# Issuing the loads of the last three parts of w_ada from GpSimd instead of SyncE

## The chip, the cores and the metric

The kernel runs on one core of a Trainium2 chip. The core has TensorE (PE, with its weight loads listed as PEld), VectorE (DVE), ScalarE (ACT), GpSimd (POOL) and SyncE (SP), which issues most DMA transfers. The metric is the device time of one execution in microseconds.

## The reference, cut to what matters

One layer of a decoder trunk on x of 1024 tokens by 1024 features. A conditioning vector c gives six vectors of 1024: shift, scale and gate of the mixer, and shift, scale and gate of the FFN.

```python
c_act = jax.nn.silu(c)
ada = c_act @ w_ada[l] + b_ada[l]                       # 1024 x 6144
sh_m, sc_m, g_m, sh_f, sc_f, g_f = jnp.split(ada, 6, axis=-1)
h = modulate(rms_norm(x), sh_m, sc_m)
proj = h @ w_in[l]
...                                                     # token shift
y_rwkv = rwkv7_time_mix(z, ...)                         # 8 heads x 64, a recurrence over the tokens
y_s5 = s5_mix(u, ...)                                   # 32 groups x 16, state space, then a GLU
mix = jnp.concatenate([y_rwkv, y_s5], axis=-1) @ w_out[l]
x = x + g_m[:, None, :] * mix
h = modulate(rms_norm(x), sh_f, sc_f)
ffn = (jax.nn.silu(h @ ffn_w_gate[l]) * (h @ ffn_w_up[l])) @ ffn_w_down[l]
x = x + g_f[:, None, :] * ffn
return rms_norm(x) * final_gain
```

Parts 0 to 2 of `ada` are shift, scale and gate of the mixer; parts 3, 4 and 5 (shift, scale and gate of the FFN) are first needed after the output projection of the first half.

## The kernel before

The tokens are worked in four quarters (`qt`) for the recurrence and in two halves for the output projection and the FFN. The recurrence of a quarter is prepared (`prepare`, `post`: decays, normed keys, the products `pA`, a triangular solve on DVE or POOL whose input goes out to `l_d` and comes back as `LU`, and whose result goes out to `x_d` and is read again before `pG`), then run as a chain of chunks (`chunk`, L1080: products `p1` to `p4`, copies `R` and `U` and the state `ST` on DVE, each needing the one before), then finished (`finishes`: a norm over each head, `pv` and `pg` on PE, result `yhl`).

The adaLN product `c_act @ w_ada` is not done on PE. w_ada is loaded with its rows over the partitions, each 128-row block is multiplied by its column of `cact` and added up in `acc` (`ada_acc`), and PE adds over the partitions (`ada_cols`, L306, tile `pac`), after which DVE adds the bias into `mod` (L307). Parts 0 to 2 are done at the start, with loads of 512 KB. Parts 3 to 5 are done by `ada_steps` in twelve steps of 256 columns. A step issues four loads of 256 KB (L285, tile `wada`, 128x2x256 elements, four buffers, so that each load waits until the step before has read the same buffer) and then adds up eight blocks. In six steps, called mixed here, ACT multiplies (L299) and POOL adds (L300), after a first multiply on DVE (L295); in the other six, which alternate with them, DVE does all eight (L295 once, L297 seven times). The column sums of a step stand two steps behind its loads.

The work around the change is woven in the source by generators that take turns. The S5 GLU (`s5_glu`: `pglu` on PE, `hl_glu`, `zhl`, `ssum` and `yhl` on POOL) and the steps of w_ada (`adg`) are written beside the chunk chains of the first two quarters, `c0` and `c1`:

```python
    weave(c0, (LIM(glg, 20), 3), LIM(adg, 12))
    ...
    weave(LIM(c1, 14), finishes(0), (glg, 1), (adg, 3))
    ads.close()
    ...
    weave(seq(c1, finishes(1)), LIM(o0, 4), LIM(late, 4))
```

`o0` is the output projection of the first half (`outproj`, L1346, PSUM tile `po`). Its four accumulators use the PSUM tags "s", "p", "A" and "G", which `pac` and the GLU use before, so it starts after the last `pac`; with it run the loads of x (L1312), of w_out (`wraw`, L1341) and of y (L1324). `late` is the recurrence of the last two quarters; after `o0` the FFN (`pgate`, `pup`, `pdn`) runs beside it.

The order in which each engine gets its instructions is not the order of the source: when the program is built, a scheduler with a model of each instruction's time orders them engine by engine. Each engine then runs its own list strictly in that order, and a queue's DMA issues stand in the list of the engine that issues them, with their waits.

Of the kernel before, what the change touches and what calls it, by code (L numbers as in the profile page):

```python
# [17 lines left out]
P = 128  # L18
# [11 lines left out]
def kernel(  # L30
# [38 lines left out]
    nc = tc.nc  # L69
    V, S, G, PE = nc.vector, nc.scalar, nc.gpsimd, nc.tensor  # L70
# [206 lines left out]
    rstd_x = const.tile([P, 8], F32, name="rstd_x")  # L277
    tcol = const.tile([P, 8], F32, name="tcol")

    def ada_load(pl, part, j0, n, bufs):  # L280
        c0 = 1024 * part + 128 * j0
        wts = []
        for kk in range(4):
            wt = pl.tile([P, 2, 128 * n], F32, tag="wada", bufs=bufs, name="wada")
            nc.sync.dma_start(wt, w_ada[0, 256 * kk:256 * kk + 256, c0:c0 + 128 * n].rearrange("(k p) n -> p k n", p=P))  # L285
            wts.append(wt)
        return wts

    def ada_acc(pl, wts, n, eng=V):

        acc = pl.tile([P, 128 * n], F32, tag="acc", bufs=2 if n > 2 else 3, name="acc")
        for k in range(8):
            wt = wts[k // 2][:, k % 2, :]
            if k == 0:
                V.tensor_scalar_mul(acc, wt, cact[:, 0:1])  # L295
            elif eng is V:
                V.scalar_tensor_tensor(out=acc, in0=wt, scalar=cact[:, k:k + 1], in1=acc, op0=ALU.mult, op1=ALU.add)  # L297
            else:
                S.mul(wt, wt, cact[:, k:k + 1])  # L299
                G.tensor_tensor(out=acc, in0=acc, in1=wt, op=ALU.add)  # L300
        return acc

    def ada_cols(acc, part, j0, n, ps):

        for j in range(n):
            PE.matmul(ps[:, j:j + 1], lhsT=acc[:, 128 * j:128 * j + 128], rhs=ones[:, 0:1], start=True, stop=True)  # L306
        V.scalar_tensor_tensor(out=mod[:, part, j0:j0 + n], in0=ps, scalar=1.0 if part in (1, 4) else 0.0,  # L307
                               in1=col("b_ada", 8 * part + j0, n), op0=ALU.add, op1=ALU.add)
# [227 lines left out]

    xts, uw = [load_x(0)], []
    wa = [ada_load(sp, part, 0, 4, 6) for part in range(2)]
    dgs = norm_x(0, xts[0])
    acs = [ada_acc(sp, w, 4) for w in wa]  # L540
    transpose_x(xts[0], dgs)
    uw += [load_u(0), load_u(1)]
    xts.append(load_x(1))
    wa = [ada_load(sp, part, 4, 4, 6) for part in range(2)]
    mods(*acs, 0)
    for b in range(4):
# [17 lines left out]
    for hf, b in ((0, 2), (0, 3), (1, 2)):  # L564
        for k in range(4):
            u_mm(hf, k, b)
    mods(*acs, 4)
    wa = [(part, j0, ada_load(sp, part, j0, 4, 6)) for part in (2,) for j0 in (0, 4)]
    for hf in range(2):
        for k in range(4, 8):  # L570
# [273 lines left out]
    def ada_steps(pl, parts, ps, mix=lambda j: j % 4):  # L844

        todo = []
        def cols():
            acc, part, j = todo.pop(0)
            ada_cols(acc, part, j, 2, ps("pac2")[:, 0:2])
        for part in parts:  # L850
            for j in (0, 2, 4, 6):
                todo.append((ada_acc(pl, ada_load(pl, part, j, 2, 4), 2, V if mix(j) else None), part, j))
                if len(todo) > 2:
                    cols()
                yield
        while todo:
            cols()
            yield
# [244 lines left out]
    def chains(qt):  # L1103
        for ch in range(4):
            gen = [chunk(q, ch, sts[qt, q]) for q in range(2)]
            for _ in range(4):
                for g in gen:
                    next(g)
                yield
# [158 lines left out]
    c0 = chains(0)  # L1268
# [7 lines left out]
    xpa = pool("xpa", stack=xs0)  # L1276
    glg = s5_glu(pool("glp", stack=gls))
    adg = ada_steps(pool("adp2", stack=ads), (3, 4, 5), ps_s)
    weave(c0, (LIM(glg, 20), 3), LIM(adg, 12))

# [239 lines left out]
```

## Time and profile before

| | us |
|---|---|
| median of 3 runs | 1576.38 |
| lowest and highest run | 1573.71, 1582.4 |
| profiled execution | 1568.54 |
| its span, first to last instruction | 1566.8 |
| PE busy | 1415.5 (90%) |
| DVE busy | 939.1 (60%) |
| ACT busy | 568.3 (36%) |
| POOL busy | 540.6 (35%) |

The profile is one execution. Busy time is the sum of an engine's instructions, without DMA issues and waits; a share of the span is a mean over stages with different limits. In the rows further down, times are microseconds from the start of the span unless marked ns, "x" counts instructions, "SPq" is SyncE issuing a transfer, and the text behind an arrow names what released a waiting instruction. The stage of `ada_steps` lies between 430 and 583 us.

### The profile page before, as it was taken

What the parts mean: (1) busy time and instruction counts of PE and PEld (TensorE: products, weight loads), DVE (VectorE), ACT (ScalarE), POOL (GpSimd) and SP (SyncE); (2) the same over time, 40 slices, a digit from 0 to 9 for tenths busy, and PEclk for the clock granted to TensorE, in tenths of its full rate; (3) what the DMA queues carried; (4) which work ended last, traced back from release to release, by engine and by line L of the source; (5) the groups of instructions that cost most, each with busy time, mean ns of one, the idle gap of its engine ahead of it and who ended that gap; (6) DMA issues with size and microseconds to landing.
All of it is one profiled execution on the core that took longest, in us unless ns stands there. A gap on an engine that the chain in (4) does not pass through costs nothing.

```text
span 1566.8 us, 23019 instructions
## 1 busy us (share of the span) xinstructions
PE 1415.5 (90%) x9071; PEld 1142.7 (73%) x9071; DVE 939.1 (60%) x1603; ACT 568.3 (36%) x928; POOL 540.6 (35%) x495
## 2 busy tenths in 40 slices
PE   3897799898968889898999999899997999999997
PEld 2776687676757658686777778777786888888885
DVE  5976328889696877754466755356637433433335
ACT  4342335454346544332143413223443322222223
POOL 4359534342163533371000005200541344544443
PEclk9898899998879859998999999999999999999999
DMA  9734555453463572344123234322822333333331
GB/s 289 227 104 141 167 175 166 115 152 96 90 167 76 148 219 81 81 102 102 45 87 98 81 91 107 85 82 76 246 82 73 116 108 94 95 94 95 108 95 54
DMA packets 261518, 184.54 MB, mean 118 GB/s; under 512 B 79767, under 2 KB 230945, under 8 KB 261409
## 3 DMA queue, kind: packets, MB, share of 16 engines
q1 hardware_dynamic: 257680, 174.85, 38.5%
q10 hardware_dynamic: 2912, 7.64, 1.4%
q8 instruction: 71, 1.16, 0.3%
q0 software_dynamic: 816, 0.57, 0.2%
q14 instruction: 39, 0.31, 0.1%
HBM read 155.53 MB, written 29.59 MB: 118 GB/s over the span
## 4 chain that ended last, share of the span: by engine, by line
PE 63%; DVE 14%; DMA 8%; POOL 7%; ACT 4%; issue 3%; SPq 1%; ACTq 0%; DVEq 0%; POOLq 0%
PE pdn L270 13%; PE pgate L270 13%; PE pup L270 13%; PE pz L270 6%; PE po L1346 5%; PE p L1080 2%; DMA wada<-in_w_ada_dram 2%; PE pu L367 2%; POOL stmp L1024 2%; POOL XU L1026 2%; DVE acc L297 2%; PE pY L765 1%; PE pA L980 1%; DMA LU<-l_d 1%; DVE stmp L1024 1%
## 5 line engine op out<-in xcount | busy, mean ns | idle before, releaser
L270 PE MATMUL pdn<-wd,act 128*128 128x512 f32 x1056 | 271.2, 398 | 0.7 <-DVE x L1395 0.5
L270 PE MATMUL pup<-h,hl_up 128*128 128x512 f32 x1056 | 265.5, 394 | 3.9 <-ACT hl_up L131 3.9
L270 PE MATMUL pgate<-h,hl_g 128*128 128x512 f32 x1056 | 263.4, 395 | 2.3 <-ACT hl_g L131 1.7
L270 PEld LDWEIGHTS pup<-h,hl_up 128*128 128x128 f32 x1056 | 197.0, 188 | 49.1 <-ACT hl_up L131 5.2
L270 PEld LDWEIGHTS pdn<-wd,act 128*128 128x128 f32 x1056 | 197.8, 190 | 46.5 <-DVE x L1395 2.1
L270 PEld LDWEIGHTS pgate<-h,hl_g 128*128 128x128 f32 x1056 | 196.7, 188 | 47.2 <-ACT hl_g L131 3.0
L1395 DVE TENSOR_TENSOR x<-pdn,x 128x512 f32<-128x512 f32 x176 | 118.8, 688 | 185.6 <-PE pdn L270 185.5
L270 PE MATMUL pz<-hT,hl_z 128*128 128x256 f32 (+1 forms) x912 | 188.3, 365 | 24.7 <-POOL hl_z L127 8.1
L270 PEld LDWEIGHTS pz<-hT,hl_z 128*128 128x128 f32 x912 | 153.6, 210 | 55.1 <-ACT zo L890 10.0
L1430 DVE TENSOR_TENSOR rawd<-rawd,gfb 128x1024 f32<-128x1024 f32 x44 | 57.1, 1297 | 91.7 <-DMA rawd<-in_ffn_w_down_dram 65.4
L1346 PE MATMUL po<-wo,yhl 128*128 128x512 f32 x384 | 95.6, 401 | 0.7 <-POOL wo L127 0.7
L131 ACT CAST hl_up<-raw_up 128x1024 fp32r<-128x1024 f32 x44 | 46.2, 1049 | 129.9 <-PE pup L270 103.3
L131 ACT CAST wd<-rawd 128x1024 fp32r<-128x1024 f32 x44 | 45.6, 1049 | 108.7 <-DVE rawd L1430 83.7
L1346 PEld LDWEIGHTS po<-wo,yhl 128*128 128x128 f32 x384 | 71.8, 190 | 18.1 <-issue 1.4
L1424 ACT ACTIVATE sgt<-pgate 128x512 f32<-128x512 f32 x44 | 26.3, 598 | 145.3 <-PE pgate L270 145.1
L1024 POOL TENSOR_TENSOR stmp<-LU,XU 128x126 f32<-128x126 f32 (+22 forms) x62 | 31.0, 500 | 129.3 <-DMA LU<-l_d 124.7
L127 POOL TENSOR_TENSOR hl_g<-raw_g,hl_g 128x1024 fp32r<-128x1024 f32 x19 | 45.6, 2398 | 79.6 <-ACT hl_g L131 75.8
L127 POOL TENSOR_TENSOR wd<-rawd,wd 128x1024 fp32r<-128x1024 f32 x19 | 49.7, 2618 | 55.9 <-ACT wd L131 55.9
L893 POOL TENSOR_TENSOR zo<-zo,zm 128x512 f32<-128x512 f32 x28 | 44.0, 1570 | 70.3 <-ACT zo L890 58.3
L127 POOL TENSOR_TENSOR hl_up<-raw_up,hl_up 128x1024 fp32r<-128x1024 f32 x19 | 49.7, 2616 | 50.6 <-ACT hl_up L131 50.6
L131 ACT CAST hl_g<-raw_g 128x1024 fp32r<-128x1024 f32 x44 | 46.0, 1045 | 48.3 <-DMA raw_g<-in_ffn_w_gate_dram 48.3
L297 DVE SCALAR_TENSOR_TENSOR acc<-wada,cact,acc 128x512 f32<-128x512 f32 (+1 forms) x84 | 62.2, 746 | 1.6 <-DMA wada<-in_w_ada_dram 0.9
(378 smaller groups left out, 2406.0 us busy)
## 6 DMA issues: line engine op xcount, KB each, us to landing
raw_g<-in_ffn_w_gate_dram SPq DMA_DIRECT2D x44, 512.0 KB, 3.9
raw_up<-in_ffn_w_up_dram SPq DMA_DIRECT2D x44, 512.0 KB, 4.3
rawd<-in_ffn_w_down_dram SPq DMA_DIRECT2D x44, 512.0 KB, 3.4
wada<-in_w_ada_dram SPq DMA_DIRECT2D x24, 512.0 KB, 8.8
raw_z<-in_w_in_dram SPq DMA_DIRECT2D x24, 512.0 KB, 5.7
wada<-in_w_ada_dram SPq DMA_DIRECT2D x48, 256.0 KB, 3.1
wraw<-in_w_out_dram SPq DMA_DIRECT2D x32, 256.0 KB, 3.2
zt_d<-zo SPq DMA_DIRECT2D x28, 256.0 KB, 2.9
```

The costliest lines, as they stand in the source:

```text
L127: (eng or G).tensor_tensor(out=out, in0=a, in1=b, op=ALU.subtract)
L131: S.copy(dst[:, 0], src)
L270: PE.matmul(ps, lhsT=lf(a, k), rhs=rf(b, k), start=(n == 0), stop=(n == 3 * kb - 1))
L297: V.scalar_tensor_tensor(out=acc, in0=wt, scalar=cact[:, k:k + 1], in1=acc, op0=ALU.mult, op1=ALU.add)
L367: PE.matmul(pu[hf, b], lhsT=uw[b][:, a_, k, :], rhs=hT[hf, k][:, b_, :], start=(k == 0 and n == 0), stop=(k == 7 and n == 2))
L893: G.tensor_tensor(out=o, in0=o, in1=zm[:, 0:HT], op=ALU.add)
L1024: SOLVE.tensor_tensor(out=t, in0=LU[:, j, j + 1:32].unsqueeze(2).to_broadcast([P, nt, nk]), in1=X[:, j:j + 1, 0:nk].to_broadcast([P, nt, n ...
L1026: SOLVE.tensor_tensor(out=X[:, j + 1:32, 0:nk], in0=X[:, j + 1:32, 0:nk], in1=t, op=ALU.add)
L1080: PE.matmul(ps[r, h], lhsT=a, rhs=b, start=(n == 0), stop=(n == len(ops) - 1))
L1346: PE.matmul(pss[i], lhsT=yh[k][:, a, 128 * i:128 * i + 128], rhs=wo[:, b], start=(k == 4 and n == 0), stop=(k == 3 and n == 2))
L1395: V.tensor_tensor(out=t, in0=ps, in1=t, op=ALU.add)
L1430: V.tensor_tensor(out=raw, in0=raw, in1=gfb, op=ALU.mult)
```

## The change

`ada_load` takes the queue as an argument, and `ada_steps` passes GpSimd's. The 24 loads of parts 0 to 2 stay on SyncE; the 48 loads of 256 KB go to GpSimd.

```diff
-    def ada_load(pl, part, j0, n, bufs):
+    def ada_load(pl, part, j0, n, bufs, q=None):
...
             wt = pl.tile([P, 2, 128 * n], F32, tag="wada", bufs=bufs, name="wada")
-            nc.sync.dma_start(wt, w_ada[0, 256 * kk:256 * kk + 256, c0:c0 + 128 * n].rearrange("(k p) n -> p k n", p=P))
+            (q or nc.sync).dma_start(wt, w_ada[0, 256 * kk:256 * kk + 256, c0:c0 + 128 * n].rearrange("(k p) n -> p k n", p=P))
...
-                todo.append((ada_acc(pl, ada_load(pl, part, j, 2, 4), 2, V if mix(j) else None), part, j))
+                todo.append((ada_acc(pl, ada_load(pl, part, j, 2, 4, nc.gpsimd), 2, V if mix(j) else None), part, j))
```

Since the scheduler orders the whole program anew, the lists of all engines change in this stage. Three places show it.

**POOL, in the second quarter's chain** (`ssum`, `zhl` and `yhl` are the GLU's). Before:

```order
L1017 MEMSET XU 128x512
L1019 MEMSET XU 64x16 x2
L127 TENSOR_TENSOR yhl<-zz,yhl 128x64x4 x4
L814 TENSOR_TENSOR ssum<-ssum,sg 128x256 x3
L127 TENSOR_TENSOR zhl<-zz,zhl 128x1024
L127 TENSOR_TENSOR yhl<-zz,yhl 128x64x4 x4
L300 TENSOR_TENSOR acc<-acc,wada 128x256
```

After:

```order
L1019 MEMSET XU 64x16 x2
L285 DMA wada<-in_w_ada_dram 128x2x256
L127 TENSOR_TENSOR zhl<-zz,zhl 128x1024
L814 TENSOR_TENSOR ssum<-ssum,sg 128x256
L127 TENSOR_TENSOR yhl<-zz,yhl 128x64x4 x4
L814 TENSOR_TENSOR ssum<-ssum,sg 128x256 x2
L127 TENSOR_TENSOR zhl<-zz,zhl 128x1024
L814 TENSOR_TENSOR ssum<-ssum,sg 128x256
L285 DMA wada<-in_w_ada_dram 128x2x256 x4
L127 TENSOR_TENSOR yhl<-zz,yhl 128x64x4 x4
L300 TENSOR_TENSOR acc<-acc,wada 128x256
```

Issues of L285, each with a wait for the reader of its buffer, stand between and ahead of the GLU's work and the adds.

**DVE, around the last state `ST` of the second quarter's chunk chain** (p_5219 is that chunk's product; the number behind `pac` tells the twelve column sums apart). Before:

```order
L297 SCALAR_TENSOR_TENSOR acc<-wada,cact,acc 128x256
L295 TENSOR_SCALAR acc<-wada,cact 128x256
L297 SCALAR_TENSOR_TENSOR acc<-wada,cact,acc 128x256 x2
L1093 TENSOR_TENSOR ST<-p_5219,ST 128x128
L1094 TENSOR_TENSOR ST<-ST,pc 128x128
L295 TENSOR_SCALAR acc<-wada,cact 128x256
L297 SCALAR_TENSOR_TENSOR acc<-wada,cact,acc 128x256
L307 SCALAR_TENSOR_TENSOR mod<-pac_4837,cols 128x2
```

After:

```order
L1093 TENSOR_TENSOR ST<-p_5219,ST 128x128
L253 SCALAR_TENSOR_TENSOR ra<-ra,rs 128x256
L1094 TENSOR_TENSOR ST<-ST,pc 128x128
L254 SCALAR_TENSOR_TENSOR rs<-ra,rs 128x256
L307 SCALAR_TENSOR_TENSOR mod<-pac_4652,cols 128x2
L295 TENSOR_SCALAR acc<-wada,cact 128x256
L830 SCALAR_TENSOR_TENSOR zz<-zz,hga,rs 128x256 x4
L297 SCALAR_TENSOR_TENSOR acc<-wada,cact,acc 128x256
```

The chain's last state stood ahead of the tenth column sum (pac_4837) and stands now ahead of the fifth (pac_4652); behind it the multiply of L295 occurred once more before, and occurs five times now.

**PE, from the last chunk products (p_5308) to the output projection.** Before:

```order
L1080 MATMUL p_5308<-ar,ST 64x64 x2
L1080 MATMUL p_5308<-ak,U 64x64 x2
L919 MATMUL pw<-wzk,wa_132 128x256 x2
L306 MATMUL pac_4837<-ones,acc 128x1 x2
L1117 MATMUL pd<-ar,cen 128x512
L919 MATMUL pa<-wzk,wa_132 128x256 x2
L306 MATMUL pac_4869<-ones,acc 128x1 x2
L1117 MATMUL pd<-ar,cen 128x512
L306 MATMUL pac_4873<-ones,acc 128x1 x2
L1124 MATMUL pv<-lsq,blk 128x512
L1346 MATMUL po<-wo,yhl 128x512 x4
```

After:

```order
L1080 MATMUL p_5308<-ak,U 64x64 x2
L306 MATMUL pac_4652<-ones,acc 128x1 x2
L967 MATMUL pb<-rz,blk 128x512
L1117 MATMUL pd<-ar,cen 128x512
L306 MATMUL pac_4687<-ones,acc 128x1 x2
L919 MATMUL pw<-wzk,wa_132 128x256 x2
L1117 MATMUL pd<-ar,cen 128x512
L306 MATMUL pac_4739<-ones,acc 128x1 x2
L919 MATMUL pa<-wzk,wa_132 128x256 x2
L1124 MATMUL pv<-lsq,blk 128x512
L306 MATMUL pac_4788<-ones,acc 128x1 x2
```

Three column sums stood between the last chunk product and the first `po`; now there are eight, the last four of them (with `pv`, `pg` four times in the list, `pgb` eight times and `pn` between) below the rows shown. Behind that, on PE in the output projection, 16 of the 64 `pA` products of the third quarter stand now ahead of the last 60 `po`, where all 64 stood behind the last `po` before.

## Rows read from the trace of the kernel before

**Rows 1.** The page, busy us (share of the span) and instructions of an engine.
```profile
PE 1415.5 (90%) x9071; PEld 1142.7 (73%) x9071; DVE 939.1 (60%) x1603; ACT 568.3 (36%) x928; POOL 540.6 (35%) x495
```

**Rows 2.** Windows: stretch, length, busy of PE, PEld, DVE, ACT, POOL, clock, DMA, GB/s.
```profile
510.00:550.00 40.00, 33.24 (x410) 25.81 (x408) 34.97 (x80) 20.95 (x44) 19.25 (x21) 0.86 0.57 155
550.00:590.00 40.00, 33.10 (x204) 22.58 (x204) 31.10 (x65) 17.77 (x37) 15.30 (x19) 0.55 0.68 215
...
630.00:670.00 40.00, 33.12 (x268) 26.80 (x267) 28.16 (x53) 12.89 (x25) 12.08 (x8) 1.00 0.36 89
...
720.00:960.00 240.00, 235.77 (x1546) 184.46 (x1545) 144.53 (x214) 76.80 (x106) 3.59 (x11) 0.99 0.31 86
```
**Rows 3.** The chain of waits, 405 to 600 us: start, us, what.
```profile
554.77 8.89 DMA wada<-in_w_ada_dram
564.66 2.74 DMA wada<-in_w_ada_dram
568.84 2.85 DMA wada<-in_w_ada_dram
```

**Rows 4.** Waits of SyncE's queue, 430 to 600 us: total, times, longest.
```profile
SPq L285 <- POOL acc L300: 25.8, 17, 4.2
...
SPq L285 <- DVE acc L297: 7.3, 6, 2.9
```

**Rows 5.** Timeline of PE, 541 to 583 us: start, duration, instruction.
```profile
549.22 1.01 PE L306 MATMUL pac<-ones,acc 128*128 128x1 f32 x4
...
566.89 0.42 PE L1080 MATMUL p<-ak,U 64*64 64x64 f32 x4
...
580.36 0.98 PE L306 MATMUL pac<-ones,acc 128*128 128x1 f32 x4
...
582.64 1.33 PE L1346 MATMUL po<-wo,yhl 128*128 128x512 f32 x1
```

**Rows 6.** The tile wada: ns min/median/max of its issues, and us to landing.
```profile
L285 SPq DMA_DIRECT2D wada<-in_w_ada_dram x72: 367/373/4237, 2.7 to 573.9; - x72
...
DMA to landing us min/median/max: 2.8/3.2/11.7
```

**Rows 7.** The tile dcol, loaded by POOL: the same columns.
```profile
L651 POOL DMA_DIRECT2D dcol<-in_s_d_dram x4: 528/536/568, 129.6 to 131.2; - x4
...
DMA to landing us min/median/max: 2.9/3.2/3.6
```

**Rows 8.** Timeline of POOL at the start of the program.
```profile
2.99 0.60 POOL L315 DMA_DIRECT2D g2w<-in_rw_g_dram  x1
```

**Rows 9.** Timeline of DVE, 128 to 133 us.
```profile
130.31 1.23 DVE L127 TENSOR_TENSOR hl_z<-raw_z,hl_z 128x1024 fp32r<-128x1024 f32 x1
```

**Rows 10.** Groups by line, 430 to 600 us: busy us, mean ns, idle before.
```profile
L300 POOL TENSOR_TENSOR acc<-acc,wada 128x256 f32<-128x256 f32 x42 | 33.7, 803 | 24.5 <-ACT wada L299 21.5 <-DVE acc L295 1.4
...
L297 DVE SCALAR_TENSOR_TENSOR acc<-wada,cact,acc 128x256 f32<-128x256 f32 x42 | 25.5, 608 | 0.4
L299 ACT ACTIVATE wada<-wada,cact 128x256 f32<-128x256 f32 x42 | 19.3, 500 | 24.5 <-DMA wada<-in_w_ada_dram 18.2 <-DVE acc L297 5.2 <-DVE zz L830 0.8
...
L295 DVE TENSOR_SCALAR acc<-wada,cact 128x256 f32<-128x256 f32 x12 | 5.5, 458 | 3.9 <-DMA wada<-in_w_ada_dram 3.9
```

**Rows 11.** Timeline of PE after the first po, 590 to 720 us.
```profile
601.18 1.02 PE L1139 MATMUL pg<-gs,g2w 128*128 128x256 f32 x4
605.71 0.61 PE L1292 MATMUL pgb<-dgb,ones 128*128 128x128 f32 x4
...
619.47 1.02 PE L939 MATMUL pn<-sq,blk 128*128 128x512 f32 x2
...
715.74 1.91 PE L1046 MATMUL pG<-XU,ak 32*32 32x32 f32 x64 [6.71 <-DMA XU<-x_d]
```

## Prediction

> **What bounds the kernel now.** I read the page first, then the busy time by stretch, then the chain of waits, then the waits of SyncE's queue, and last the rows of TensorE where the stage of w_ada ends. The page says that PE is busy 90% of the span [rows 1], but that is a mean. From 720 us on PE works 235.8 of 240 us [rows 2], so what is late there stays late to the end. In 510 to 590 us it works 33.2 and 33.1 of each 40 us, at a granted clock of 0.86 and then 0.55, while DVE works 35.0 of the 40 us up to 550 [rows 2]. That earlier stretch is where the change lies, and there PE waits for others. The chain of waits names the loads of w_ada in it: the three longest pieces at its end are 8.89, 2.74 and 2.85 us [rows 3], the last ahead of the output projection. The queue's own waits say why: before issuing a load of L285 SyncE stood 25.8 us for adds of GpSimd (17 times) and 7.3 us for DVE (6 times), because each of the four buffers has to be read before the next load may fill it [rows 4].
>
> So there are two chains side by side: the twelve steps of w_ada (load, multiply and add, column sums, `mod`), and the chunk chain of the second quarter (L1080). The first output projection `po` takes PSUM tags that the column sums `pac` use, so it starts only after the last `pac`. Its time is the number to forecast. Before, the chunk chain's last group starts at 566.89 us, the last `pac` at 580.36 and the first `po` at 582.64 [rows 5]: 15.75 us from the first of these to the last.
>
> **The change part by part.** The 48 issues leave SyncE. Each costs SyncE 0.37 us (minimum and median 367 and 373 ns), the long ones being waits [rows 6]. That is 48 x 0.37 = 18 us of an engine with nothing else to compute, beside other work: worth nothing by itself. What the queue kept behind it (x, kz, rz, wraw) comes sooner. From the trace that is worth between nothing and the 8.89 us piece [rows 3], whose landing fell beside those loads; I take nothing, as a load that comes sooner has to find PE ready, and below the order says it does not.
>
> GpSimd gets 48 issues. Its other loads are the nearest rows: 0.60 us for the 256 KB of g2w, 528 to 568 ns for the four of dcol, which land in 2.9 to 3.6 us (median 3.2), against 2.8 and 3.2 us for wada on SyncE [rows 6 to 8]. So I take 0.6 us to issue and an unchanged 3.2 us to land. GpSimd now also waits for DVE's release of a buffer before issuing, and what is queued behind it waits too: the adds of the mixed steps (42 of 0.80 us each [rows 10]) and the GLU's `hl_glu`, `ssum`, `zhl` and `yhl`, for which PE and ACT wait.
>
> *The pace of the steps.* A pair is one mixed step and one step on DVE alone. GpSimd pays 8 x 0.6 + 7 x 0.80 = 10.4 us a pair. One buffer's round is two issues and two landings (7.6 us), two DVE operations (1.2 us at 608 ns), an ACT multiply (0.5) and two adds (1.6): 10.9 us [rows 6, 7, 10]. So 5.2 to 5.5 us a step at best. The measured pace before is from the `pac` at 549.22 to that at 580.36, five steps apart: 31.1 / 5 = 6.2 us [rows 5]. I take 6.2, since queueing in the order given comes on top of the bare sums, and keep 5.2 as the lower end.
>
> *What moves behind the chunk chain.* This is the main term, and it comes from the order, not from the queue. The scheduler put the steps of w_ada later against the chunk chain. On DVE, after the chain's last `ST`, before had one and a half steps to go and after has five and a half: four more. On PE three of the twelve `pac` stood after the last L1080 and now eight do. Nothing but small work is left for PE there, so each of these steps is exposed: 4 x 6.2 = 24.8 us (20.8 by the low pace, 31.0 with five steps).
>
> *What the chunk chain gains.* The DVE work of those four steps no longer delays it: two steps of 0.46 + 7 x 0.608 = 4.7 us and two single multiplies of 0.46, 10.3 us [rows 10]. DVE was busy 87% of the time there, so most of it counts, but GpSimd's waits hold the GLU that PE runs in between. Ends: 0 and 10.3 us; I take 7. The chain's last group then starts near 560 us.
>
> *Sum at the first* `po`: 566.9 - 7 + 15.75 + 24.8 = 600.4 us, against 582.64: 17.8 us later.
>
> *What is given back.* While PE waits in the longer tail, it does work that stood behind or among `po` before: `pg` twice 1.02 us, sixteen `pgb` at 0.61 us for four (2.4 us), and `pn` 1.02 us [rows 11]: 5.5 us. Further on PE waited 6.71 us for the solve before `pG` at 715.74 [rows 11]. Preparation for that solve (`pn`, `pb`, a quarter of `pA`) stands earlier against `po` now, so part of this wait goes: from nothing to all, and I take half, 3.4 us. PE's idle 6.9 us in 630 to 670 [rows 2] I leave as it is: the chain from the last `po` through the norm to the first `pgate` still runs there. It is kept for the range. Net: 17.8 - 5.5 - 3.4 = 8.9 us.
>
> The profiled execution took 1568.54 us, its span 1566.8, and stands 7.8 us (0.5%) below the median of 1576.38. The sum against its own time is 1577.4; against the median, 1576.4 + 8.9 = 1585.
>
> The Trainium skill, "DMA: Bandwidth & Descriptors", section "Issuing engines are not separate DMA queues", says that issuing from another engine saves only the issuing time, as all transfers run on the same 16 DMA engines. The landings agree (3.2 us on either path). By that rule alone the change would be worth about nothing; the order's shift is what it leaves out.
>
> **Rivals.**
> *A, given back in full.* The tail is as late as I say or a little less, but the 6.71 us and the 6.9 us of idle PE time go as well, since the preparation runs ahead of `po`. 17.8 - 5.5 - 6.7 - 5 = +0.6 us: 1577. For it: `pA` now starts within `po`. Against it: the wait in 630 to 670 lies partly in DVE and GpSimd work that follows the last `po`.
>
> *B, faster.* The tail is short: the chain ends at 556.6 (all 10.3 us gained) and the four steps take 5.2 us each, so `po` starts at 556.6 + 15.75 + 20.8 = 593.2, 10.5 us late; with 5.5, 6.7 and 5 us given back that is -6.7, and with SyncE's loads early (2.8 us, one landing) about -9: 1567. For it: the waits of SyncE [rows 4] are gone. It decides if the last `pac` comes before about 591 us.
>
> *C, GpSimd's issue is dear.* An issue has to wait until DVE's operation of the moment is done. DVE works 78% of 550 to 590 us (31.1 of 40 [rows 2]) in operations of 0.6 us and more [rows 10], so each issue could take 0.6 us more: 4 issues a step, 2.4 us a step, over the five and a half steps in the tail 13 us more: +22 us, 1598. Against it: the four issues of dcol, from 129.55 us on, all took 528 to 568 ns [rows 7], while DVE ran operations of 1.23 us on 128x1024 elements [rows 9]. It decides if the median issue without its wait is above 1 us. The Trainium skill, "SBUF — State Buffer", section "SBUF: two separate sides", states the mechanism of C: GpSimd writes the descriptors itself and is locked out while DVE runs certain two-port operations; its example goes from about 620 to about 3100 ns. By its figures an issue would cost 2.5 us more, and the sum several tens of us; no row here shows that.
>
> *D, the change does not do what it says* (the loads still on SyncE's queue): the order shows 48 of them on GpSimd, so I give it no weight.
>
> **How the numbers follow.** About 0.5% (8 us) is what a measurement here can tell from no change: faster is below 1568.5, slower above 1584.3. Forecast 0.46, of which 0.35 lies above that bound and 0.11 within; A 0.26, of which 0.24 within and 0.02 below; B 0.16, below; C 0.12, above. So faster 0.18, same 0.35, slower 0.47. The range has to reach A and most of B and C: 1566 at the lower end (B), and at the upper end the sum with five steps and the chunk chain not earlier, 566.9 + 15.75 + 31.0 = 613.7, 31 us late, less 5.5: +25.5, so 1602. The forecast's own range is 1577 to 1593.
>
> **What the profile after would show.** The last L1080 of the second quarter near 560 us (556 to 567); the first `po` near 600 (593 to 614) and after the eighth `pac`; five spacings of `pac` of about 6 us each with PE mostly idle; GpSimd's issues of L285 at about 0.6 us plus waits for DVE; landings near 3.2 us; the wait before `pG` shorter than 6.7 us; PE busy as before from 720 us on. Wrong if `po` starts before 591 us (the tail was hidden), if a bare issue is above 1 us (C), or if `po` is some 18 us late and the end is not (A).

## The result, and the profile after

The changed kernel takes 1612.18 us (median of 4 runs, 1610.82 to 1613.05) against 1579.39 us for the kernel before on the same chip: a ratio of 1.0234, 95% interval 1.0202 to 1.0266. It is 2.3% slower. The forecast was 1585 us, slower too, but the time lies above the whole range (1566 to 1602). The profiled execution took 1612.16 us with a span of 1610.4 us, 43.6 us more than the span of before. The sum had found 8.9 us of that.

The page after, with the line that answers to [rows 1], the line of GpSimd's DMA queue and the line of the loads (KB each, median us to landing):

```profile
span 1610.4 us, 23015 instructions
PE 1437.3 (89%) x9071; PEld 1155.3 (72%) x9071; DVE 950.6 (59%) x1603; ACT 571.2 (35%) x930; POOL 576.4 (36%) x543
q0 software_dynamic: 4656, 13.16, 2.9%
wada<-in_w_ada_dram POOLq DMA_DIRECT2D x48, 256.0 KB, 3.5
```

PE's busy time grew by 21.8 us from [rows 1] with the same 9071 matmuls, nearly all of it in one stretch at a granted clock of 0.50, the lower of its two levels (below); the rest is waiting. By the medians the loss is 32.8 us. The profiled execution of before was a quick one, 10.9 us under the median of its four runs, and that of the changed kernel lies on its median; so about a quarter of the 43.6 us that the traces differ by is spread between executions, and where it lies the traces don't tell. To find the place of the rest, I lined up the same five events in both traces (us from the start of the span):

| event | before | after | later by |
|---|---|---|---|
| solve of the second quarter starts (DVE L1024) | 433.50 | 439.10 | 5.6 |
| its result reaches PE (`pG`) | 478.94 | 485.95 | 7.0 |
| last group of L1080 of that quarter | 566.89 | 571.41 | 4.5 |
| first `po` | 582.64 | 626.81 | 44.2 |
| end | 1566.8 | 1610.4 | 43.6 |

So 39.65 us come up between the last L1080 and the first `po`, and of the 44.2 us by which `po` is late all but 0.6 us reach the end. TensorE's timeline after in that tail (start, length, line, tiles, idle before it and its releaser) answers to [rows 5]:

```profile
571.41 0.42 PE L1080 MATMUL p<-ak,U 64*64 64x64 f32 x4
571.76 1.01 PE L306 MATMUL pac<-ones,acc 128*128 128x1 f32 x4
...
595.37 2.08 PE L1139 MATMUL pg<-gs,g2w 128*128 128x256 f32 x4 [3.03 <-DVE lsq L1125]
603.96 2.08 PE L1139 MATMUL pg<-gs,g2w 128*128 128x256 f32 x4 [6.52 <-DVE ld L1140]
605.83 0.85 PE L306 MATMUL pac<-ones,acc 128*128 128x1 f32 x4
...
621.87 1.01 PE L306 MATMUL pac<-ones,acc 128*128 128x1 f32 x4 [0.66 <-POOL acc L300]
625.22 0.99 PE L306 MATMUL pac<-ones,acc 128*128 128x1 f32 x4 [2.34 <-DVE acc L297]
626.81 0.77 PE L1346 MATMUL po<-wo,yhl 128*128 128x512 f32 x1 [0.60 <-DVE mod L307]
```

Eight `pac` stand behind the last L1080, as the order had said. From the first of them to the last are 53.46 us, 7.64 us a step. The longest waits of PE there end on DVE. The tail by engine (stretch, length, then busy us and instructions of PE, PEld, DVE, ACT and POOL, granted clock, DMA share, GB/s), first before, then after, each with the time from the first `po` to the end behind it:

```profile
566.90:582.60 15.70, 12.62 (x34) 6.83 (x32) 9.15 (x22) 11.08 (x24) 5.22 (x7) 0.50 0.63 185
582.60:1566.80 984.20, 940.76 (x5384) 758.28 (x5382) 515.09 (x747) 308.87 (x468) 286.60 (x242) 0.98 0.33 95
```

```profile
571.40:626.80 55.40, 32.46 (x85) 19.77 (x83) 45.24 (x90) 24.45 (x47) 29.35 (x38) 0.50 0.54 162
626.80:1610.40 983.60, 941.32 (x5354) 756.94 (x5354) 500.15 (x710) 299.81 (x455) 284.07 (x242) 0.98 0.33 95
```

In the tail PE's busy time grew from 12.62 to 32.46 us, at a clock of 0.50 in both, and DVE is busy 45.24 of 55.4 us. Its costliest groups there (operation, tiles, count, busy us, mean ns, idle before):

```profile
L297 DVE SCALAR_TENSOR_TENSOR acc<-wada,cact,acc 128x256 f32<-128x256 f32 x21 | 11.3, 538 | 2.9 <-DMA wada<-in_w_ada_dram 2.6
L1291 DVE TENSOR_SCALAR dgb<-ident,mod 128x128 f32<-128x128 f32 x8 | 4.1, 526 | 1.0 <-PE pgb L1292 0.8
L253 DVE SCALAR_TENSOR_TENSOR lsq<-lsq,lrs 128x512 f32<-128x512 f32 x2 | 2.9, 1440 | 0.0
L1133 DVE SCALAR_TENSOR_TENSOR lrs<-lrs,cols,bo 128x256 f32<-128x256 f32 x4 | 2.8, 707 | 0.0
L295 DVE TENSOR_SCALAR acc<-wada,cact 128x256 f32<-128x256 f32 x5 | 2.2, 448 | 1.5 <-DMA wada<-in_w_ada_dram 1.5
```

Only L297 and L295, 13.5 us, are adds of w_ada. With 1.2 us of `mod` taken off too, 30.5 us belong to other work: finishing the second quarter (`lsq`, `lrs`, `yhl`), preparing the third, and `dgb`. It stands between the steps in DVE's list, so a step whose load has landed waits for it.

The loads after, and GpSimd's longest wait before one (us in total, times, longest), which answer to [rows 6] and [rows 4]:

```profile
L285 POOL DMA_DIRECT2D wada<-in_w_ada_dram x48: 722/722/762, 427.7 to 620.3; - x48
...
POOL wada L285 <- DVE acc L297: 29.6, 11, 10.5
```

An issue takes 0.72 us and hardly varies. These 48 loads land in 3.1/3.5/8.0 us (least, median, most), where before they landed in 2.8/3.1/4.4; the 3.2 of [rows 6] is over all 72 loads of w_ada, 24 of them of 512 KB. The waits that SyncE had for buffers now stand in GpSimd's list, but for DVE: 29.6 us where SyncE had 7.3.

### The profile page after: what moved, and what is told of

Read it like the earlier page. It is cut to its first block, busy times and chain, and to the rows that moved or that the text cites. A ratio compares the mean times of both kernels' runs of the same rounds, so it can differ in the third digit from the quotient of the medians.

```text
span 1610.4 us, 23015 instructions
## 1 busy us (share of the span) xinstructions
PE 1437.3 (89%) x9071; PEld 1155.3 (72%) x9071; DVE 950.6 (59%) x1603; ACT 571.2 (35%) x930; POOL 576.4 (36%) x543
## 3 DMA queue, kind: packets, MB, share of 16 engines
q10 hardware_dynamic: 2912, 7.64, 1.4%
## 4 chain that ended last, share of the span: by engine, by line
PE 62%; DVE 14%; POOL 7%; DMA 6%; issue 4%; ACT 4%; SPq 1%; ACTq 0%; DVEq 0%; POOLq 0%
PE pdn L270 13%; PE pgate L270 13%; PE pup L270 13%; PE pz L270 6%; PE po L1346 4%; PE p L1080 3%; POOL XU L1026 2%; POOL stmp L1024 2%; PE pu L367 2%; DVE acc L297 1%; PE pY L765 1%; DMA LU<-l_d 1%; PE pA L980 1%; DVE stmp L1024 1%; PE pglu L270 1%
## 5 line engine op out<-in xcount | busy, mean ns | idle before, releaser
L1346 PE MATMUL po<-wo,yhl 128*128 128x512 f32 x384 | 95.0, 402 | 1.5 <-POOL wo L127 0.9
L1346 PEld LDWEIGHTS po<-wo,yhl 128*128 128x128 f32 x384 | 73.2, 193 | 18.8 <-POOL wo L127 2.1
L1024 POOL TENSOR_TENSOR stmp<-LU,XU 128x126 f32<-128x126 f32 (+22 forms) x62 | 27.8, 448 | 124.9 <-DMA LU<-l_d 120.4
L127 POOL TENSOR_TENSOR yhl<-yt,yhl 128x512 fp32r<-128x512 f32 (+1 forms) x12 | 18.1, 1516 | 132.1 <-ACT yhl L1331 125.0
```

Of the source, the lines that this page charges most:

```text
L127: (eng or G).tensor_tensor(out=out, in0=a, in1=b, op=ALU.subtract)
L1024: SOLVE.tensor_tensor(out=t, in0=LU[:, j, j + 1:32].unsqueeze(2).to_broadcast([P, nt, nk]), in1=X[:, j:j + 1, 0:nk].to_broadcast([P, nt, n ...
L1346: PE.matmul(pss[i], lhsT=yh[k][:, a, 128 * i:128 * i + 128], rhs=wo[:, b], start=(k == 4 and n == 0), stop=(k == 3 and n == 2))
```

## The experiments

The change does two things at once: it moves 48 issues to another queue, and since the scheduler orders the program anew, it changes the order of every engine's list. The first question is which of them costs. For that an order can be forced: the names of the instructions of this stage, engine by engine as the list of one kernel has them, are written into another, and each instruction is tied to the one before it by a dependency without a semaphore (in the diff, `seen` leads from a name to its instruction). It concerns 3050 instructions of PE, DVE, ACT and GpSimd. Below, "old order" means the lists of the kernel before, "new order" those of the changed kernel. In short (us; the last three columns from the profiled execution):

| loads of w_ada, order | median | ratio to before, 95% | last L1080 | first `po` | `po` to end |
|---|---|---|---|---|---|
| SyncE, old (kernel before) | 1579.4 | | 566.9 | 582.6 | 984.2 |
| GpSimd, new (the change) | 1612.2 | 1.0234 [1.0202, 1.0266] | 571.4 | 626.8 | 983.6 |
| e1: GpSimd, old | 1595.1 | 1.0124 [1.0076, 1.0171] | 591.2 | 610.0 | 983.8 |
| e2: SyncE, new | 1612.0 | 1.0249 [1.0200, 1.0298] | 574.7 | 624.6 | 985.5 |
| e3: ACT, the scheduler's own | 1596.4 | 1.0148 [1.0098, 1.0197] | 580.7 | 622.4 | 981.7 |
| e4: SyncE, new on DVE alone | 1616.6 | 1.0268 [1.0219, 1.0317] | 585.5 | 636.9 | 987.3 |
| e5: e1, first step on SyncE | 1595.0 | 1.0110 [1.0067, 1.0154] | 586.3 | 604.9 | 988.1 |
| e6: ACT, old | 1580.0 | 1.0031 [1.0008, 1.0053] | 574.3 | 591.1 | 985.7 |
| e7: SyncE, old, five buffers | 1570.1 | 0.9975 [0.9948, 1.0002] | 568.4 | 583.2 | 985.0 |
| e8: SyncE, late steps alone | 1629.6 | 1.0331 [1.0286, 1.0375] | 579.8 | 621.0 | 1008.2 |
| e9: GpSimd for DVE's steps, old | 1588.3 | 1.0090 [1.0059, 1.0121] | 587.2 | 604.1 | 986.9 |
| e10: GpSimd for mixed steps, old | 1585.7 | 1.0062 [1.0037, 1.0088] | 581.2 | 598.2 | 985.8 |
| e11: SyncE, old, GpSimd kept busy | 1582.4 | 1.0050 [1.0032, 1.0068] | 576.3 | 592.2 | 988.3 |
| e12: SyncE, order of the source | 1713.9 | 1.0889 [1.0855, 1.0923] | 617.1 | 627.2 | 1076.0 |

Each ratio is to runs of the kernel before on the same chip, whose medians lie between 1572.8 and 1579.4 us. The profiled executions of e3 and e4 are each some 9 us above their medians, that of e9 4.5 above and that of e12 9 below, so their rows tell where the time lies rather than how much.

### The new order with the old queue

```diff
+ORDER = "<DVE>;<ACT>;<PE>;<POOL>"
...
+        for row in ORDER.split(";"):
+            row = ["I-" + n for n in row.split(",")]
+            for was, now in zip(row, row[1:]):
+                tc.add_manual_dep(seen[now], was, how, reason="order")
```

> The loads are back on SyncE, but TensorE, VectorE, ScalarE and GpSimd's computing instructions are held to the order of the changed kernel. Theory ORDER: slower like the changed kernel, 1600 to 1612 us, first po at 615 us or later. Theory QUEUE: as the kernel before, 1574 to 1585 us. If both count: between, 1585 to 1600.

It took 1612.04 us, as much as the changed kernel. The end of the chunk chain, the first `po`, the tail and the time behind it in its trace:

```profile
574.66 0.42 PE L1080 MATMUL p<-ak,U 64*64 64x64 f32 x4
...
624.56 2.05 PE L1346 MATMUL po<-wo,yhl 128*128 128x512 f32 x4 [0.60 <-DVE mod L307]
...
574.70:624.60 49.90, 32.19 (x85) 20.16 (x81) 41.78 (x92) 24.62 (x48) 13.77 (x17) 0.50 0.59 179
624.60:1610.10 985.50, 942.38 (x5354) 757.41 (x5354) 496.51 (x710) 299.66 (x455) 285.17 (x242) 0.98 0.33 95
```

DVE is as busy in the tail as after, and GpSimd is down from 29.35 to 13.77 us. The tail is 5.5 us shorter than after, but the chunk chain ends 3.3 us later and the time behind `po` is 1.9 us longer, so nothing is left of it at the end. So the order alone makes the whole loss, and once it is given, the queue is worth nothing.

### The old order with the new queue

```diff
-... ada_load(pl, part, j, 2, 4) ...
+... ada_load(pl, part, j, 2, 4, nc.gpsimd) ...
+ORDER = "<DVE>;<ACT>;<PE>;<POOL>"
```

The lists are those of before; the 48 issues stand in GpSimd's where the scheduler puts them between its other work.

> The loads stay on GpSimd, but TensorE, VectorE, ScalarE and GpSimd's computing instructions are held to the order of the kernel before (only where GpSimd's 48 issues and SyncE's other loads fall is left to the scheduler). Theory ORDER (the 33 us come from the twelve steps standing later against the chunk chain): most of it returns, 1575 to 1588 us, first po within 10 us of 583. Theory QUEUE (GpSimd's issues, 0.72 us each with waits in its list, and their later landing cost the time in any order): 1600 us or more, because the chunk chain now waits for the steps ahead of it.

It took 1595.1 us, 1.2% more than before and between the ranges of the two theories. Its rows:

```profile
438.71 0.19 DVE L1024 TENSOR_TENSOR stmp<-LU,XU 128x31 f32<-128x31 f32 x1 [5.62 <-DMA LU<-l_d]
...
591.22 0.42 PE L1080 MATMUL p<-ak,U 64*64 64x64 f32 x4
...
609.97 1.33 PE L1346 MATMUL po<-wo,yhl 128*128 128x512 f32 x1
...
POOL wada L285 <- DVE acc L297: 11.8, 6, 3.9
```

The tail is short again (18.75 us), but the chunk chain ends 24.3 us later than before. Solve and `pG` bring 10.8 us of that, the chain itself 13.6 (101.5 us from `pG` to the last L1080, against 88.0). So GpSimd's queue has a price of its own in the old order, some 20 us. It doesn't come on top of the order's price: the change pays 2.3% in all, and e2 without the queue as much.

### ACT's queue, in the scheduler's order and in the old one

```diff
-... ada_load(pl, part, j, 2, 4) ...
+... ada_load(pl, part, j, 2, 4, nc.scalar) ...
```

> The 48 loads are issued by ScalarE instead (a hardware queue like SyncE's, but also the list of an engine that computes); the scheduler orders anew, with six column sums behind the chunk chain instead of eight. Theory ORDER: between, by two steps of 7.6 us fewer in the tail, about 1595 us. Theory QUEUE with the cost in GpSimd's issue and landing (0.72 and 3.6 us): near the kernel before, 1575 to 1585 us.

It took 1596.35 us, as theory ORDER had it. Here too the scheduler moved steps of w_ada behind the chunk chain (six `pac`), and the tail is 41.7 us. The same queue with the lists of before forced as in e1:

> Old order, loads issued by ScalarE (hardware queue, 0.37 us an issue). If what e1 lost is GpSimd's own price (0.72 us an issue, landing 3.4 us): near the kernel before, 1573 to 1582. If it is that a computing engine's list holds the waits of the issues, and its work stands behind them: 1588 to 1597 like e1.

It took 1580.01 us, 0.3% more than before (ten runs). The loads and the two events in its trace:

```profile
L285 ACTq DMA_DIRECT2D wada<-in_w_ada_dram x48: 374/375/852, 427.2 to 582.8; - x48
...
574.27 0.42 PE L1080 MATMUL p<-ak,U 64*64 64x64 f32 x4
...
591.13 1.33 PE L1346 MATMUL po<-wo,yhl 128*128 128x512 f32 x1
```

So a computing engine's queue need not cost 20 us. ACT pays 0.375 us an issue, half of GpSimd's 0.72, and most of e1's loss is GpSimd's own.

### DVE's list alone

```diff
+ORDER = "<DVE, new order>"
```

> The loads on SyncE as before; only VectorE's list is held to the order of the changed kernel, the other engines are ordered anew around it. If VectorE's list is what makes the tail long (theory DVE: between the last chunk state and the last column sum it has to do about 36 us of work more than before, whoever loads w_ada): 1600 to 1612 us, first po at 615 us or later, VectorE busy over 80% from the last L1080 to it. If the other engines' lists or the queue matter as much: 1585 or less.

It took 1616.59 us, as slow as with all four lists and a little above the range. The tail:

```profile
585.50:636.90 51.40, 28.66 (x85) 17.41 (x83) 40.41 (x92) 24.03 (x46) 12.26 (x15) 0.57 0.57 169
```

DVE's list is enough, though the scheduler orders the other engines anew around it. What remained was why: because the steps come late in it, or because of the other work between them.

```diff
-ORDER = "<DVE, new order>"
+ORDER = "<DVE, new order, some 30 operations of finishing and preparation moved behind the last column sum>"
```

> Loads on SyncE; VectorE's list is that of the changed kernel up to the last chunk state, with the same five and a half steps of w_ada behind it (eight column sums behind the last L1080), but some 30 operations of the second quarter's finishing and the third quarter's preparation that stood between those steps are moved behind the last column sum, as the kernel before has them. Theory DVE LIST (the tail is long because VectorE does both): the tail falls from 50 us (e2) to 30 to 38 us, and the time to 1590 to 1600. Theory LATE STEPS (the five late steps alone take 7.5 us each by their own round of load, multiply, add): tail and time stay at 50 us and 1605 or more.

It took 1629.63 us, slower still, so the expected time was missed. The two stretches:

```profile
579.80:621.00 41.20, 15.73 (x57) 9.90 (x53) 22.59 (x54) 14.95 (x31) 10.98 (x15) 0.58 0.69 210
621.00:1629.20 1008.20, 951.72 (x5382) 762.97 (x5382) 512.95 (x747) 309.02 (x468) 284.67 (x242) 0.97 0.33 93
```

The tail falls to 41.2 us, with its `pac` 5.55 us apart, and DVE is busy only 22.59 us in it. That is close to the tail that the prediction had summed (40.55 us), and it is about what the late steps make by themselves. The work taken out of it was not free: behind `po` it costs 24 us (1008.2 against 984.2). About half of that lies ahead of the next `pG`, where PE stands 10.0 us for DVE's `rz`, which comes behind the work that was moved. So of the changed kernel's 55.4 us, about 41 are the late steps, and the 9 (e2) to 14 (after) above that go with the other work among them. DVE is busy 84% of the tail in e2 and 55% in e8, whose chain of waits there runs through five landings of w_ada instead, 17.1 us together.

### What GpSimd's queue costs in the old order

Three suspicions: the waits for buffers in GpSimd's list, the first loads falling beside the round trip of the solve (`LU`), and the plain time of 48 issues. For the first, half the loads were moved, once those of the steps that DVE does alone, once those of the mixed ones:

```diff
-... ada_load(pl, part, j, 2, 4, nc.gpsimd) ...
+... ada_load(pl, part, j, 2, 4, nc.gpsimd if mix(j) else None) ...
```

> Old order; only the 24 loads of the six steps on VectorE are issued by GpSimd (their buffers are released by GpSimd's own adds, so its list waits for itself), the other 24 by SyncE. If e1's 15 to 20 us are GpSimd's time per issue (0.72 us): half of it, 1580 to 1585. If they are the waits for VectorE in GpSimd's list: about nothing, 1573 to 1578.

```diff
-... ada_load(pl, part, j, 2, 4, nc.gpsimd) ...
+... ada_load(pl, part, j, 2, 4, None if mix(j) else nc.gpsimd) ...
```

> Old order; only the 24 loads of the six mixed steps are issued by GpSimd (their buffers are released by VectorE, for which GpSimd's list then waits), the other 24 by SyncE. If e1's loss is GpSimd's time per issue: half of it, 1580 to 1585, as e9. If it is the waits for VectorE in GpSimd's list: nearly all of it, 1588 to 1595.

They took 1588.33 and 1585.71 us, 0.9 and 0.6% more than before, both above the range for the theory of the time per issue, the second by less than 1 us. The one half costs three quarters of e1's 1.2%, the other half of it, and the two intervals overlap. In GpSimd's list 5.8 us are put down to waits for DVE's adds in e9 and 16.4 in e10, yet e10 is not the dearer one. The theory that the loss is mainly these waits falls with that. For the solve:

```diff
-... ada_load(pl, part, j, 2, 4, nc.gpsimd) ...
+... ada_load(pl, part, j, 2, 4, nc.gpsimd if (part, j) != (3, 0) else None) ...
```

> As e1 (loads on GpSimd, old order), but the four loads of the first step on SyncE again. In e1 and in the changed kernel these four start at 426 to 428 us, right ahead of the load LU that the second quarter's solve waits for, and the solve starts 15.0 and 14.2 us after pG of the first quarter, against 10.7 before and 9.9 in e2. Theory COLLISION (those four loads take the DMA engines from LU): 10 to 11 us again, and 4 to 5 us off e1's time, 1590. Theory ISSUE (GpSimd's issues and waits hold the GLU and the adds): no change against e1, 1593 to 1597.

In the trace the solve starts when it did in the kernel before:

```profile
433.54 0.19 DVE L1024 TENSOR_TENSOR stmp<-LU,XU 128x31 f32<-128x31 f32 x1 [0.62 <-DMA LU<-l_d]
```

From `pG` of the first quarter it is 10.7 us, as before, against 15.0 in e1 and 14.2 in the changed kernel. e9 and e10 agree: 9.5 us with the first step on SyncE and 15.2 with it on GpSimd. So the first four loads do hold up `LU` by some 4 us when GpSimd issues them, and `po` comes 5 us sooner than in e1. The median did not follow: 1595.03 us against 1595.1, where 1590 was expected. In the profiled execution 4 us more than in e1 went between `po` and the end, and whether the collision costs time is inconclusive.

For the issues' plain time the loads went back to SyncE, and GpSimd got, at each place in its list where e1 has an issue, the clearing of a tile of 128x688 that nobody reads:

```diff
             nc.sync.dma_start(wt, ...)
+            if n == 2:
+                nc.gpsimd.memset(pl.tile([P, 688], F32, tag="scr", bufs=1, name="scr"), 0.0)
```

> Loads on SyncE, old order, and GpSimd's list is e1's word for word except that each of the 48 issues is replaced by a MEMSET of a spare 128x688 tile, some 0.7 us of GpSimd's time with no wait for VectorE and no transfer. Theory OCCUPANCY (what e1 lost is GpSimd's time for 48 issues, 35 us of it, in front of the adds and the GLU's work): like e1, 1586 to 1597. Theory WAITS AND LANDING (its waits for VectorE, the later landing): like the kernel before, 1573 to 1580.

It took 1582.38 us, 0.5% more than before and between the ranges of the two theories. The clearings and the two events (L1084 and L1350 are L1080 and L1346 moved by four lines):

```profile
L288 POOL MEMSET scr<- x48: 661/672/736, 426.9 to 584.9; 128x688 f32 x48
...
576.25 0.42 PE L1084 MATMUL p<-ak,U 64*64 64x64 f32 x4
...
592.23 2.69 PE L1350 MATMUL po<-wo,yhl 128*128 128x512 f32 x4
```

So keeping GpSimd busy for nearly as long as the issues do (0.67 us against 0.72 each), without a transfer and without a wait for DVE, costs about 8 us. That is part of e1's 20. The other 12 may come from loads that go later, by the waits for buffers in GpSimd's list (11.8 us for DVE), and from the solve. No run shows which, and that stays open.

### Five buffers, and the order of the source

```diff
-... ada_load(pl, part, j, 2, 4) ...
+... ada_load(pl, part, j, 2, 5) ...
```

> Loads on SyncE, old order, five buffers in place of four, so that one load of each step need not wait for the step before. If the waits for the buffers set the pace of the steps in the kernel before (16 to 19 us of its chain of waits are landings of wada): 3 to 8 us faster, 1565 to 1571. If the chunk chain or VectorE sets it: no change.

With SyncE's queue and the old order it took 1570.07 us over ten runs, a ratio of 0.9975 whose interval reaches 1.0002. That is no difference that can be told from none, so what a fifth buffer takes away of SyncE's waits [rows 4] had cost at most some 0.5%.

```diff
-    with _tile.TileContext(nc, schedule_with_timeline_sim=True) as tc:
+    with _tile.TileContext(nc) as tc:
```

> Loads on SyncE; the whole program ordered by the scheduler without its model of times, nearly as the source is written, which puts all but one of the twelve column sums ahead of the last L1080. If the steps' place against the chunk chain were all that counts, the first po would come within 5 us of the last L1080 and the time would be that of the kernel before or better, 1560 to 1578. If the work that the old order puts beside po (VectorE's and ScalarE's) then stands ahead of it, or other stages lose by the plainer order: 1590 or more.

Without the scheduler's model of time, only one `pac` stands behind the last L1080 and `po` follows 10 us after it (617.10 and 627.18 us in the profile). Yet it took 1713.88 us, 1.0889 [1.0855, 1.0923]. Early steps alone make no fast kernel: here the chunk chain ends 50 us later than before, and 92 us more go behind `po`. As this order changes every stage, the run gives the steps' place no price.

## Why the prediction was wrong, step by step

**Where the change lies: right.** The time is lost between the chunk chain and the first `po`, through the order, and not through the transfers. e2 shows it: the old queue with the new order takes the same time as the change.

**The chunk chain: wrong sign, 11.5 us.** It was to end 7 us earlier, near 560. It ended at 571.41, 4.5 us later. The chain itself is 2.5 us shorter (85.5 us from `pG` to the last L1080, against 88.0), so the work taken from DVE brought little of its 10.3 us. It began 7.0 us later, and for that there was no term. Of these, 2.1 us are there at the first quarter's `pG` (424.91 against 422.79 us), before any of these loads goes out. From there to the solve it is 3.5 us more. The first load goes out at 427.7 us, where before it went at 440.6, after the solve had started; in the old order e5 puts some 4 us of such a delay down to these loads beside the transfer of `LU`. But the new order is as late without them. In e2, with the first load at 440.6 us, the first quarter's `pG`, the solve and its `pG` are:

```profile
426.74 1.20 PE L1046 MATMUL pG<-XU,ak 32*32 32x32 f32 x64 [2.47 <-DMA XU<-x_d]
436.66 0.19 DVE L1024 TENSOR_TENSOR stmp<-LU,XU 128x31 f32<-128x31 f32 x1 [0.50 <-DMA LU<-l_d]
486.63 1.20 PE L1046 MATMUL pG<-XU,ak 32*32 32x32 f32 x64
```

The solve isn't held up there (9.9 us), `pG` is 7.7 us later than before all the same, and the chain behind it takes 88.0 us, as before. So the gain of 7 us that the sum took didn't come with the new order, and why the chain starts late in it stays open.

**The tail: right in kind, mis-sized by 14.85 us.** Forecast 24.8 us longer, measured 39.65. Number and place of the steps were right (eight `pac` behind the chain). The term for each step was not: 6.2 us were taken over from the stretch up to the last `pac` before; here a step takes 7.64 us. The two stretches, first before (five steps) with DVE's adds of w_ada in it, then after (seven):

```profile
549.22:580.36 31.14, 24.37 (x180) 16.82 (x179) 25.28 (x58) 12.79 (x29) 10.92 (x15) 0.50 0.79 248
L297 DVE SCALAR_TENSOR_TENSOR acc<-wada,cact,acc 128x256 f32<-128x256 f32 x18 | 9.8, 546 | 0.2
L295 DVE TENSOR_SCALAR acc<-wada,cact 128x256 f32<-128x256 f32 x4 | 1.4, 352 | 3.9 <-DMA wada<-in_w_ada_dram 3.9
571.76:625.22 53.46, 31.11 (x75) 18.61 (x73) 43.33 (x86) 23.70 (x45) 28.99 (x38) 0.50 0.56 167
```

DVE is busy 81% of both, at the same clock of TensorE. But before, 11.9 us of its work belong to the steps (L297, L295 and `mod`) and 13.4 to other things, 2.7 us a step; after it is 14.5 and 28.8 us, 4.1 us of other work a step. That is 1.4 us more for each step, as much as the step is longer. e8 makes about the forecast's tail, 41 us, by clearing DVE's list between the steps. So what the sum left out is that DVE has more to do between the steps behind the chain (30.5 us in the whole tail) than where the pace was read, which the order shows in DVE's list. The pace of a step has to be worked out from everything in the list, not from the step's own operations.

**What is given back: 0.6 us instead of 8.9.** This was the third miss, of 8.3 us. With the others the account closes: 8.9 + 11.5 + 14.85 + 8.3 = 43.6. The mechanism was half right: `pg`, `pgb` and `pn` do run in the tail, and the wait before `pG` [rows 11] does go:

```profile
751.15 1.20 PE L1046 MATMUL pG<-XU,ak 32*32 32x32 f32 x64 [0.40 <-DMA XU<-x_d]
```

Stretches from the first `pgate` to `pG` of the third quarter, and from there to the end, first before, then after:

```profile
661.60:715.70 54.10, 47.42 (x231) 37.95 (x231) 23.80 (x33) 17.68 (x28) 35.05 (x66) 0.97 0.49 115
715.70:1566.80 851.10, 821.21 (x4721) 662.55 (x4721) 429.17 (x608) 258.88 (x380) 226.53 (x158) 0.98 0.33 96
```

```profile
708.00:751.10 43.10, 42.47 (x190) 33.41 (x190) 18.25 (x23) 13.35 (x19) 32.46 (x63) 0.96 0.42 108
751.10:1610.40 859.30, 825.84 (x4730) 665.28 (x4730) 434.85 (x611) 260.74 (x382) 227.50 (x158) 0.98 0.33 95
```

From the first `po` to that `pG` after is 8.8 us shorter (124.3 against 133.1). But `pG` to the end is 8.2 us longer. `pG` comes sooner against the FFN, so more of the FFN is left behind it. The three groups of FFN matmuls that stand behind `pG`, first before, then after:

```profile
L270 PE MATMUL pdn<-wd,act 128*128 128x512 f32 x1025 | 262.7, 398 | 0.7 <-DVE x L1395 0.5
L270 PE MATMUL pup<-h,hl_up 128*128 128x512 f32 x984 | 247.3, 394 | 3.9 <-ACT hl_up L131 3.9
L270 PE MATMUL pgate<-h,hl_g 128*128 128x512 f32 x974 | 242.3, 394 | 1.7 <-ACT hl_g L131 1.7
```

```profile
L270 PE MATMUL pdn<-wd,act 128*128 128x512 f32 x1034 | 265.0, 397 | 1.7 <-DVE x L1395 1.6
L270 PE MATMUL pup<-h,hl_up 128*128 128x512 f32 x986 | 249.0, 394 | 3.7 <-ACT hl_up L131 3.7
L270 PE MATMUL pgate<-h,hl_g 128*128 128x512 f32 x984 | 245.7, 396 | 2.9 <-ACT hl_g L131 2.9
```

Together 752.3 us before and 759.7 after: 7.4 of the 8.2 us. So a wait taken away ahead of `pG` was work moved to the other side of it. Over the whole time from `po` to the end PE is as busy as before (940.76 and 941.32 us), though some 5.5 us of work and four `pv` had gone ahead. The records agree with that: 5354 matmuls against 5384, and the 30 that are fewer are 16 `pgb`, 8 `pg`, 4 `pv` and 2 `pn`. Why PE is busy as long for fewer of them I can't show in full. Part may be the clock at the start of the projection: in its first 10 us 0.67 was granted, against 0.82 before. In all kernels but e8 and e12 the time from `po` to the end lies between 981.7 and 988.3 us, whatever happened before it. Nothing late is won back there.

**The rivals.** A (all given back) fails with that. B (faster) fails, as `po` came at 626.81 us and not before 591. C (a dear issue) names the wrong engine for the right sign: an issue takes 0.72 us, under its point of 1 us, though DVE is busy for 82% of the tail. By the Trainium skill, "SBUF — State Buffer", section "SBUF: two separate sides", GpSimd's writing of descriptors is locked out while DVE runs certain operations; these 48 issues, 722 to 762 ns, don't show it. Their longest landing is 8.0 us, against 4.4 before, and no run shows whether that has to do with it.

**The range.** Its upper end rested on five steps instead of four, and on an unchanged chunk chain. Its tail was still only 46.75 us, for want of the added work on DVE, and it took 5.5 us as given back for certain. By the traces' whole difference, 43.6 us on 1576.4, it would have had to reach 1620.

The Trainium skill, "DMA: Bandwidth & Descriptors", section "Issuing engines are not separate DMA queues", says that issuing from several engines saves only the time that issuing takes, as all transfers run on the same 16 DMA engines. In the new order the runs agree that the engine doesn't matter (e2 and the change within 0.2%). In the old order it does: the 48 issues, 35 us of GpSimd's time, cost 20 us of the kernel's, of which e11 puts some 8 down to the time itself.

## What to carry to other kernels

Where a scheduler orders the program, a change of one queue is a change of every engine's list: run the old queue in the new order before explaining anything by the queue. The pace of a chain in its new place follows from all that stands in the list of its busiest engine there, not from the pace that it had elsewhere. And before counting a removed wait as won, look at what ran beside it and must now run later.

## What was not expected of the hardware

GpSimd's issue of 256 KB of w_ada takes 0.722 us, with nearly no spread, where ACT takes 0.375 (e6) and SyncE 0.370 us for the same transfer (medians) and GpSimd itself 0.60 us for the 256 KB of g2w [rows 8]. The landings of these 48 loads differ little by their medians: 3.5, 3.4 and 3.1 us on GpSimd, ACT and SyncE.
